# One matmul for the compressed-attention values, ScalarE writing the probabilities, heads of a sparse group spawned 8.5 apart

## The chip, the cores and the metric

The kernel runs on one core of one Trainium2 chip. TensorE (PE in the profile) multiplies, with a separate record for its weight loads (PEld); VectorE (DVE) and ScalarE (ACT) do the elementwise work, GpSimd (POOL) a little of it, and SyncE (SP) issues the loads. The metric is the device time of one execution in microseconds; lower is better.

## What is computed

A two-layer decoder on 256 tokens of width 2048. Layer 0 is a sparse attention (NSA) with 16 heads in 4 groups, layer 1 a differential attention; each is followed by a squared-ReLU MLP. The change touches only the sparse attention, whose head mixes three softmaxes. Cut to them:

```
kc, vc = compress(k_c, 0), compress(v_c, 1)        # 15 compressed keys and values per group
s_c = einsum(qr, kc) * scale                        # q without rope
p_c = masked_softmax(s_c, cmp_end <= t)
o_c = einsum(p_c, vc)
s_s = einsum(qo, k_g) * scale                       # q with rope, selected keys
p_s = masked_softmax(s_s, valid_s);  o_s = einsum(p_s, v_g)
p_w = masked_softmax(einsum(qo, kw) * scale, valid_w);  o_w = einsum(p_w, vw)
return g[..., 0:1] * o_c + g[..., 1:2] * o_s + g[..., 2:3] * o_w
```

With 256 tokens and 16 blocks to choose, all blocks are selected, so no gather is left in the kernel.

## The kernel before, in words

Every matrix product is made of three TensorE products of float32r parts: a value is split into a high part `h` (a rounded copy that ScalarE writes) and a low part `l` (VectorE: value minus `h`), and `mm3` computes hh + hl + lh. `split` is the helper (L150 to L156); weights go through it too (`raw` to `wh` and `wl`, L152 and L153, 128x1024 each).

The order of PE and SP is written by the program itself (`manual_schedule`, L158): the order in which the Python code emits matmuls is the order in which TensorE runs them. ACT, DVE and POOL get theirs from the framework's scheduler. The emission is driven by a small planner: `clock` is a number that each emitted matmul raises by its columns / 2400, tasks are generators in a heap, `yield d` puts a task back at clock + d, and `tick()`, which stands behind every few projection matmuls, runs a task that is due. So a head is a generator whose pieces are set between projection matmuls, and `WAIT_A` (L25) holds how far apart the planner puts them.

A sparse head (`nsa_head`, L597) has four pieces on PE:
- Q: four 128x128 transposes of its q without and with rope into one PSUM bank (tag `tp`); ACT writes `qth`, DVE `qtl`.
- S: the scores, 12 matmuls that read `qth` (the third reads `qtl`), into two `tp` banks. DVE adds the mask and takes the maxima (six operations, L632), ACT takes six exponentials with their sums (L635), DVE works out the gated reciprocals `den` and multiplies the six pieces by them (L641).
- P: eight transposes of the probabilities into two `tp` banks; ACT and DVE split them into `psh`, `psl` (first bank) and `pwh`, `pwl` (second).
- O: 15 matmuls into one `tp` bank; ACT and DVE split the result into `oth` and `otl` (tiles `big`).

Slots limit how many heads can be between two pieces: `s_q` 2 (Q to S), `s_s` 2 (S to P), `s_p` 1 (P to O). There are four `tp` banks, and all pieces use them. `heads` (L673) spawns the four heads of a group `WAIT_A[3]` apart; a group is spawned `WAIT_A[4]` after its q projection. The q projections of the four groups, and behind them the output projection (`out_proj`), supply the matmuls that stand between the pieces: 128x512, tiles `acc`, reading `wh` or `wl`.

The compressed values: `compress_tail` (L528) for `j == 1` makes each group's 15 (padded to 32) values four times over the 128 partitions, and splits them into `vch` and `vcl`. In O, three matmuls use partitions 96 to 127 of these (`cr`), against the same partitions of `psh`/`psl`, where the transposed compressed probabilities stand (the transposes of `sB[:, 160:288]` and `sB[:, 192:320]` end in those 32 columns).

Of the kernel before, what the change touches and what calls it, by code (L numbers as in the profile page):

```python
# [9 lines left out]
F32 = mybir.dt.float32  # L10
# [5 lines left out]
P = 128  # L16
# [5 lines left out]
NEG = -3.0e38  # L22
FLOOR = -1.0e38

WAIT_A = (2.0, 12.5, 4.0, 1.5, 7.0)  # L25

WAIT_B = (1.0, 8.5, 5.0, 5.5, 9.0, 7.0)
LAMBDA_INIT = 0.8 - 0.6 * math.exp(-0.3 * 1)
# [3 lines left out]
def kernel(  # L32
# [43 lines left out]
    def T(shape, tag, dt=F32):  # L76
        return (sm if tag in SMALL else sb).tile(shape, dt, tag=tag, name=name(tag), bufs=BUFS[tag])
# [23 lines left out]
    def spawn(gen, delay=0.0):  # L101
        task = Task(gen)
        put(task, delay)
        return task
# [32 lines left out]
    def mm(o, l, r, start, stop, shared=False):  # L137
        nc.tensor.matmul(o, lhsT=l, rhs=r, start=start, stop=stop, skip_group_check=shared)  # L138
        clock[0] += max(o.shape[-1], 256) / 2400.0
# [5 lines left out]
    def mm3(o, lh, ll, rh, rl, start, stop):  # L145
        mm(o, lh, rh, start, False)
        mm(o, lh, rl, False, False)
        mm(o, ll, rh, False, stop)

    def split(h, l, src, scale=None):  # L150
        if scale is None:
            nc.scalar.activation(h, src, AF.Copy)  # L152
            nc.vector.tensor_tensor(l, src, h.bitcast(F32), ALU.subtract)  # L153
        else:
            nc.scalar.activation(h, src, AF.Copy, scale=scale)
            nc.vector.scalar_tensor_tensor(l, src, scale, h.bitcast(F32), ALU.mult, ALU.subtract)  # L156
# [327 lines left out]
    def make_gates():  # L484
# [16 lines left out]
        nc.vector.tensor_scalar(gates, gates, 1.0, None, ALU.add)  # L501
        nc.vector.reciprocal(gates, gates)

    tG = spawn(make_gates())
    drain(tG)
    w2t = T([P, 2, 4, P], "q")
# [3 lines left out]

    kch = cp.tile([P, P], F32R, name="kch")
    kcl = cp.tile([P, P], F32R, name="kcl")
    vch = cp.tile([P, 4, P], F32R, name="vch")
    vcl = cp.tile([P, 4, P], F32R, name="vcl")

    def cmp_units(j, cps, first):
        def f(u):
# [10 lines left out]
    def compress_tail(cps, j):  # L528
        hs = T([120, 512], "sa")
        nc.scalar.activation(hs, cps[0:120, :], AF.Copy)  # L530
        yield 1.5
        tp = PT("tp")
        for k in range(4):
            transpose(tp[:, k * 120:(k + 1) * 120], hs[:, k * P:(k + 1) * P],
                                ident[0:120, 0:120])
        tv = tp[:, 0:480].rearrange("p (k c) -> p k c", k=4)
        u = T([P, 4, 60], "pwh")
        v = T([P, 4, 60], "pwl")
        nc.scalar.activation(v, tv[:, :, 60:120], AF.Copy)
        nc.vector.tensor_tensor(u, tv[:, :, 0:60], v, ALU.add)  # L540
        nc.gpsimd.tensor_tensor(v, u, u, ALU.mult)
        nc.vector.tensor_scalar(v, v, 0.044715, 1.0, ALU.mult, ALU.add)
        nc.gpsimd.tensor_tensor(v, v, u, ALU.mult)
        nc.scalar.activation(v, v, AF.Tanh, scale=math.sqrt(2.0 / math.pi))
        nc.vector.tensor_scalar(v, v, 1.0, None, ALU.add)
        gel = T([P, 4, 4, 32], "psh")
        nc.vector.memset(gel, 0.0)
        nc.gpsimd.tensor_tensor(gel.rearrange("p k h n -> p (k h) n")[:, :, 0:15],
                                u.rearrange("p k (h n) -> p (k h) n", n=15),
                                v.rearrange("p k (h n) -> p (k h) n", n=15), ALU.mult)  # L550
        gvs = []
        if j == 1:
            for h, tag in enumerate(("sa", "sa", "psl", "pwh")):
                gv = T([P, 4, 4, 32], tag)
                nc.gpsimd.tensor_copy(gv, gel[:, :, h, None, :].to_broadcast([P, 4, 4, 32]))
                gvs.append(gv)
        yield 10.0 if j == 0 else 16.0
        if j == 0:
            tp = PT("tp")
            for k in range(4):  # L560
                mm(tp[:, 0:128], w2[0][:, k, :], gel[:, k].rearrange("p h n -> p (h n)"), k == 0, k == 3)
            split(kch, kcl, tp[:, 0:128], half)
        else:
            tp = PT("tp")
            for h in range(4):
                gv = gvs[h]
                for k in range(4):
                    mm(tp[:, h * P:(h + 1) * P], gv[:, k].rearrange("p r n -> p (r n)"),
                       w2[1][:, k, :], k == 0, k == 3)
            split(vch.rearrange("p h d -> p (h d)"), vcl.rearrange("p h d -> p (h d)"), tp, half)  # L570

    half = cp.tile([P, 1], F32, name="half")
    nc.gpsimd.memset(half, 0.5)
# [23 lines left out]
    def nsa_head(hd, qr, qo):  # L597
        g, i = hd // 4, hd % 4
        yield from s_q.take()
        tp = PT("tp")  # L600
        for s_, src in ((0, qr), (2, qo)):
            for t in range(2):
                transpose(tp[:, (s_ + t) * P:(s_ + t + 1) * P], src[:, t, i * P:(i + 1) * P], ident)
        qh = T([P, 4, P], "qth", F32R)
        ql = T([P, 4, P], "qtl", F32R)
        split(qh.rearrange("p a q -> p (a q)"), ql.rearrange("p a q -> p (a q)"), tp)
        yield WAIT_A[0]
        yield from s_s.take()
        A = PT("tp")
        mm3(A, qh[:, 3, :], ql[:, 3, :], kkh[:, g], kkl[:, g], True, True)  # L610
        B = PT("tp")
        mm3(B[:, 0:256], qh[:, 2, :], ql[:, 2, :], kkh[:, g, 0:2], kkl[:, g, 0:2], True, True)
        n = slice(g * 32, (g + 1) * 32)
        mm3(B[:, 256:288], qh[:, 0, :], ql[:, 0, :], kch[:, n], kcl[:, n], True, True)
        mm3(B[:, 288:320], qh[:, 1, :], ql[:, 1, :], kch[:, n], kcl[:, n], True, True)
        s_q.give()
        sA = T([P, 512], "sa")
        sB = T([P, 320], "sbt")
        mx = T([P, 6], "mx")
        den = T([P, 6], "den")  # L620
        sv = sA.rearrange("p (a q) -> p a q", a=4)
        Av = A.rearrange("p (a q) -> p a q", a=4)
        spec = [
            (1, sB[:, 0:128], B[:, 0:128], cmask[:, 128:256], 1),
            (2, sB[:, 128:256], B[:, 128:256], cmask[:, 128:256], 2),
            (0, sB[:, 256:288], B[:, 256:288], vmask[:, 0:32], 0),
            (3, sB[:, 288:320], B[:, 288:320], vmask[:, 32:64], 0),
            (4, sv[:, 0::2, :], Av[:, 0::2, :], cm2, 1),
            (5, sv[:, 1::2, :], Av[:, 1::2, :], cm2, 2),
        ]  # L630
        for ix, so, si, mk, _ in spec:
            nc.vector.tensor_tensor_reduce(so, si, mk, 1.0, FLOOR, ALU.add, ALU.max, mx[:, ix:ix + 1])  # L632
        nc.vector.tensor_scalar(mx, mx, -scA, None, ALU.mult)
        for ix, so, si, mk, _ in spec:
            nc.scalar.activation(so, so, AF.Exp, bias=mx[:, ix:ix + 1], scale=scA, accum_out=den[:, ix:ix + 1])  # L635
        nc.vector.tensor_scalar(den, den, 1e-30, None, ALU.max)
        nc.vector.reciprocal(den, den)
        dv = den.rearrange("p (t b) -> p t b", t=2)
        nc.vector.tensor_tensor(dv, dv, gates[:, :, hd * 3:hd * 3 + 3], ALU.mult)
        for ix, so, si, mk, _ in spec:  # L640
            nc.vector.tensor_scalar(so, so, den[:, ix:ix + 1], None, ALU.mult)  # L641
        yield WAIT_A[1]
        yield from s_p.take()
        pts = []
        for br, srcs in enumerate((
            (sB[:, 0:128], sA[:, 0:128], sB[:, 160:288], sB[:, 192:320]),
            (sB[:, 128:256], sA[:, 128:256], sA[:, 384:512], sA[:, 256:384]),
        )):
            tp = PT("tp")
            for s_, src in enumerate(srcs):  # L650
                transpose(tp[:, s_ * P:(s_ + 1) * P], src, ident)
            ph = T([P, 512], ("psh", "pwh")[br], F32R)
            pl = T([P, 512], ("psl", "pwl")[br], F32R)
            split(ph, pl, tp)
            pts.append((ph, pl))
        s_s.give()
        yield WAIT_A[2]
        o = PT("tp")
        ds = slice(g * P, (g + 1) * P)
        cr = slice(96, 128)  # L660
        (ph, pl), (wph, wpl) = pts
        mm3(o[:, 0:256], vvh[:, 0, 0, ds], vvl[:, 0, 0, ds], ph[:, 0:256], pl[:, 0:256], True, False)
        mm3(o[:, 0:256], vch[cr, g, :], vcl[cr, g, :], ph[cr, 256:512], pl[cr, 256:512], False, False)
        mm3(o[:, 0:256], vvh[:, 1, 0, ds], vvl[:, 1, 0, ds], wph[:, 0:256], wpl[:, 0:256], False, False)
        mm3(o[:, 128:256], vvh[:, 1, 1, ds], vvl[:, 1, 1, ds], wph[:, 256:384], wpl[:, 256:384], False, False)
        mm3(o[:, 128:256], vvh[:, 0, 1, ds], vvl[:, 0, 1, ds], wph[:, 384:512], wpl[:, 384:512], False, True)
        s_p.give()
        split(oth[:, hd, :], otl[:, hd, :], o[:, 0:256])
# [364 lines left out]
```

## Time and profile before

| | |
|---|---|
| time, median of 3 runs (lowest to highest) | 2153.72 us (2153.3 to 2156.54) |
| the profiled execution: time, span | 2155.18 us, 2153.4 us |
| PE busy | 2127.6 us (99%), 10780 matmuls |
| DVE busy | 1334.7 us (62%) |
| ACT busy | 1082.9 us (50%) |
| chain that ended last | PE 93%, DVE 3%, DMA 1%, ACT 1% |
| mean DMA rate | 183 GB/s |

Busy is the share of the span in which an engine had an instruction running. Consecutive instructions of PE, ACT and DVE overlap in the records, so what one matmul costs the engine is read from the start of one to the start of the next, and not from its length. The sparse heads lie between about 222 and 402 us of the span, the heads of the differential attention between about 1237 and 1397 us.

### The profile page before, as it was taken

The numbers are of one execution on the slowest core, as the hardware profiler recorded it, in microseconds if no ns is written. First come the engines' busy times: TensorE is split into PE (matmuls) and PEld (weight loads), VectorE is DVE, ScalarE is ACT, GpSimd is POOL, SyncE is SP. The second block draws the span as 40 slices with busy tenths as digits, with TensorE's granted clock in tenths as the row PEclk, the third lists the DMA queues.
The fourth block names the chain that finished last, engine by engine and source line by source line (L and its number), as shares of the span: only waits on it lengthen the run. The fifth ranks groups of instructions, "written<-read, shape, count | busy, mean of one in ns | idle before, by whom it ended". The sixth has DMA issues, their size and how long they took to land.

```text
span 2153.4 us, 28803 instructions
## 1 busy us (share of the span) xinstructions
PE 2127.6 (99%) x10780; PEld 1796.6 (83%) x10780; DVE 1334.7 (62%) x2156; ACT 1082.9 (50%) x1737; POOL 81.3 (4%) x121
## 2 busy tenths in 40 slices
PE   8999999999999999999999999999999999999998
PEld 6878888888888888888888877888888888888886
DVE  5666777675556556655666578866546555655654
ACT  6665666464435434434555466654434434534443
POOL 0101100000000000000000111000000000000000
PEclk9999999999999999999999999999999999999999
DMA  7787433456666666666665543466566666666654
GB/s 241 238 271 242 128 98 95 149 172 191 191 190 190 196 195 185 196 191 191 188 190 187 188 138 126 128 191 190 190 193 185 195 195 189 187 200 187 194 192 142
DMA packets 204828, 394.45 MB, mean 183 GB/s; under 512 B 14176, under 2 KB 14368, under 8 KB 204560
## 3 DMA queue, kind: packets, MB, share of 16 engines
q1 hardware_dynamic: 203936, 390.51, 58.2%
q0 software_dynamic: 560, 2.02, 0.3%
q8 instruction: 84, 1.38, 0.3%
q14 instruction: 56, 0.46, 0.1%
q10 hardware_dynamic: 192, 0.08, 0.0%
HBM read 390.47 MB, written 2.10 MB: 182 GB/s over the span
## 4 chain that ended last, share of the span: by engine, by line
PE 93%; DVE 3%; DMA 1%; ACT 1%; issue 1%; POOL 0%; SPq 0%; POOLq 0%; DVEq 0%; ACTq 0%
PE acc L138 58%; PE tp L138 33%; PE tp L142 2%; DMA raw<-in_nsa_cmp_w_dram 1%; DVE wl L153 1%; ACT wh L152 1%; DMA raw<-in_nsa_w_in_dram 0%; ACT sbt L884 0%; ACT sa L884 0%; POOL sq L920 0%; DVE sbt L891 0%; DVE big L156 0%; DVE psl L153 0%; DVE sa L891 0%; DVE pwl L916 0%
## 5 line engine op out<-in xcount | busy, mean ns | idle before, releaser
L153 DVE TENSOR_TENSOR wl<-raw,wh 128x1024 fp32r<-128x1024 f32 x736 | 903.5, 1229 | 703.9 <-ACT wh L152 699.4
L152 ACT ACTIVATE wh<-raw 128x1024 fp32r<-128x1024 f32 x736 | 778.5, 1059 | 819.3 <-PE acc L138 478.8
L138 PE MATMUL acc<-wh,big 128*128 128x512 f32 (+1 forms) x1600 | 543.2, 400 | 1.5 <-ACT wh L152 1.5
L138 PE MATMUL acc<-wh,kv 128*128 128x512 f32 x1280 | 397.2, 390 | 0.0
L138 PE MATMUL tp<-big,wh 128*128 128x512 f32 (+1 forms) x1040 | 359.5, 392 | 0.0
L138 PE MATMUL acc<-big,wh 128*128 128x512 f32 x1024 | 358.1, 394 | 0.0
L138 PEld LDWEIGHTS acc<-wh,big 128*128 128x128 f32 (+1 forms) x1600 | 301.6, 189 | 60.9 <-ACT wh L152 1.9
L138 PE MATMUL acc<-wl,big 128*128 128x512 f32 (+1 forms) x832 | 326.3, 392 | 0.5 <-DVE wl L153 0.5
L138 PE MATMUL tp<-big,wl 128*128 128x256 f32 (+1 forms) x1040 | 288.9, 280 | 0.0
L138 PE MATMUL acc<-big,wl 128*128 128x256 f32 x1024 | 286.9, 280 | 0.0
L138 PEld LDWEIGHTS acc<-wh,kv 128*128 128x128 f32 x1280 | 240.3, 188 | 50.0
L138 PE MATMUL acc<-wl,kv 128*128 128x512 f32 x640 | 249.0, 389 | 0.0
L138 PE MATMUL tp<-wh,kv 128*128 128x512 f32 x768 | 237.4, 389 | 0.0
L138 PEld LDWEIGHTS tp<-big,wh 128*128 128x128 f32 (+1 forms) x1040 | 194.2, 187 | 44.0
L138 PEld LDWEIGHTS acc<-big,wh 128*128 128x128 f32 x1024 | 192.3, 188 | 43.7
L138 PEld LDWEIGHTS tp<-big,wl 128*128 128x128 f32 (+1 forms) x1040 | 194.9, 188 | 0.0
L138 PEld LDWEIGHTS acc<-big,wl 128*128 128x128 f32 x1024 | 193.0, 188 | 0.2
L138 PEld LDWEIGHTS acc<-wl,big 128*128 128x128 f32 (+1 forms) x832 | 157.1, 189 | 28.6 <-DVE wl L153 1.0
L138 PEld LDWEIGHTS tp<-wh,kv 128*128 128x128 f32 x768 | 144.1, 188 | 29.9
L138 PE MATMUL tp<-wl,kv 128*128 128x512 f32 x384 | 149.4, 389 | 0.0
L138 PEld LDWEIGHTS acc<-wl,kv 128*128 128x128 f32 x640 | 120.2, 188 | 24.5
L152 ACT ACTIVATE kv<-q 128x256 fp32r<-128x256 f32 x128 | 50.0, 412 | 73.5 <-DVE q L745 73.5
(183 smaller groups left out, 1418.5 us busy)
## 6 DMA issues: line engine op xcount, KB each, us to landing
raw<-in_mlp_w_up_dram SPq DMA_DIRECT2D x256, 512.0 KB, 3.9
raw<-in_mlp_w_down_dram SPq DMA_DIRECT2D x256, 512.0 KB, 4.0
raw<-in_nsa_w_in_dram SPq DMA_DIRECT2D x80, 512.0 KB, 4.5
raw<-in_nsa_cmp_w_dram SPq DMA_DIRECT2D x32, 512.0 KB, 5.0
raw<-in_nsa_w_out_dram SPq DMA_DIRECT2D x32, 512.0 KB, 3.7
raw<-in_diff_w_q_dram SPq DMA_DIRECT2D x32, 512.0 KB, 3.7
raw<-in_diff_w_out_dram SPq DMA_DIRECT2D x32, 512.0 KB, 3.7
raw<-in_kv_w_shared_dram SPq DMA_DIRECT2D x16, 512.0 KB, 3.6
```

What stands on the lines that cost most here:

```text
L138: nc.tensor.matmul(o, lhsT=l, rhs=r, start=start, stop=stop, skip_group_check=shared)
L142: nc.tensor.transpose(o, i, idn)
L152: nc.scalar.activation(h, src, AF.Copy)
L153: nc.vector.tensor_tensor(l, src, h.bitcast(F32), ALU.subtract)
```

## The change

It has four parts. The spacing of a group's heads in the planner, `WAIT_A[3]`, becomes 8.5 in place of 1.5. ACT's exponential of the compressed scores reads each score four times over and writes 4 x 32 columns (`sc`), its sum is four times as large, and the gate of that branch is multiplied by 4 once. The compressed values are kept in one tile `vcs` whose partitions hold h, l, h, l in blocks of 32, and the transposed probabilities hold their high part in partitions 0 to 63 and their low part in 64 to 127: one matmul over 128 partitions takes the place of three over 32. The split of that bank is written out: one copy by ACT, two subtractions by DVE (128x256, and 64x256 in place).

```
-WAIT_A = (2.0, 12.5, 4.0, 1.5, 7.0)
+WAIT_A = (2.0, 12.5, 4.0, 8.5, 7.0)
...
+        gc = gates.rearrange("p t (h b) -> p t h b", b=3)[:, :, :, 0]
+        nc.vector.tensor_scalar(gc, gc, 4.0, None, ALU.mult)
...
-    vch = cp.tile([P, 4, P], F32R, name="vch")
-    vcl = cp.tile([P, 4, P], F32R, name="vcl")
+    vcs = cp.tile([P, 4, P], F32R, name="vcs")
...
-            split(vch.rearrange("p h d -> p (h d)"), vcl.rearrange("p h d -> p (h d)"), tp, half)
+            vf = vcs.rearrange("p h d -> p (h d)")
+            nc.scalar.activation(vf, tp, AF.Copy, scale=half)
+            for r in (slice(32, 64), slice(96, 128)):
+                nc.vector.scalar_tensor_tensor(vf[r], tp[r], half[r], vf[r].bitcast(F32), ALU.mult, ALU.subtract)
...
-        sB = T([P, 320], "sbt")
+        sB = T([P, 576], "sbt")
+        sc = sB[:, 256:512].rearrange("p (t r n) -> p t r n", t=2, r=4)
...
-        for ix, so, si, mk, _ in spec:
-            nc.scalar.activation(so, so, AF.Exp, bias=mx[:, ix:ix + 1], scale=scA, accum_out=den[:, ix:ix + 1])
+        es = []
+        for ix, so, si, mk, br in spec:
+            if br == 0:
+                so, eo = so[:, None, :].to_broadcast([P, 4, 32]), sc[:, ix // 3]
+            else:
+                eo = so
+            es.append((ix, eo))
+            nc.scalar.activation(eo, so, AF.Exp, bias=mx[:, ix:ix + 1], scale=scA, accum_out=den[:, ix:ix + 1])
...
-        for ix, so, si, mk, _ in spec:
-            nc.vector.tensor_scalar(so, so, den[:, ix:ix + 1], None, ALU.mult)
+        for ix, eo in es:
+            nc.vector.tensor_scalar(eo, eo, den[:, ix:ix + 1], None, ALU.mult)
...
-            (sB[:, 0:128], sA[:, 0:128], sB[:, 160:288], sB[:, 192:320]),
+            (sB[:, 0:128], sA[:, 0:128], sB[:, 256:384], sB[:, 384:512]),
...
-            split(ph, pl, tp)
+            if br == 0:
+                nc.scalar.activation(ph, tp, AF.Copy)
+                nc.vector.tensor_tensor(pl[:, 0:256], tp[:, 0:256], ph[:, 0:256].bitcast(F32), ALU.subtract)
+                lo = ph[64:128, 256:512]
+                nc.vector.tensor_tensor(lo, tp[64:128, 256:512], lo.bitcast(F32), ALU.subtract)
+            else:
+                split(ph, pl, tp)
...
-        mm3(o[:, 0:256], vch[cr, g, :], vcl[cr, g, :], ph[cr, 256:512], pl[cr, 256:512], False, False)
+        mm(o[:, 0:256], vcs[:, g, :], ph[:, 256:512], False, False)
```

The first place is PE in the last sparse head: in the order before, its Q is `tp_3538` and its S begins with `tp_3711`; `acc` rows are projection matmuls.

```order
L142 MATMUL tp_3538<-cst,q_3139 128x128 x2
L142 MATMUL tp_3538<-cst,q_3142 128x128 x2
L138 MATMUL acc_3269<-wh_3404,big_1616 128x512
...
L142 MATMUL tp_3690<-cst,sbt_3493 128x128
...
L138 MATMUL acc_3646<-wh_3531,big_1617 128x512
L138 MATMUL tp_3711<-kv_611,qth_3543 128x512
L138 MATMUL tp_3711<-kv_612,qth_3543 128x512
```

The same head in the order now: Q is `tp_3629`, S begins with `tp_3663`, and P of the head before it (`tp_3641`, `tp_3651`) stands between them.

```order
L142 MATMUL tp_3629<-cst,q_3124 128x128 x2
L142 MATMUL tp_3629<-cst,q_3127 128x128 x2
L138 MATMUL acc_3286<-wh_3475,big_1616 128x512
L138 MATMUL acc_3286<-wl_3476,big_1616 128x512
L138 MATMUL acc_3286<-wh_3475,big_1617 128x512
L142 MATMUL tp_3641<-cst,sbt_3442 128x128
...
L142 MATMUL tp_3651<-cst,sa_3441 128x128 x3
L138 MATMUL acc_3287<-wh_3475,big_1616 128x512
L138 MATMUL acc_3287<-wl_3476,big_1616 128x512
L138 MATMUL acc_3287<-wh_3475,big_1617 128x512
L138 MATMUL tp_3663<-kv_611,qth_3634 128x512
```

In the order before, 88 rows lie between this head's Q and its S, now 11. S of the last head was at row 1705 and is now at row 1658; S of the first was at 878 and is now at 879.

The second place is ACT around the same head's `qth`, first before:

```order
L635 ACTIVATE sbt_3493,den_3495<-sbt_3493,mx_3494 128x128 x2
L635 ACTIVATE sbt_3493,den_3495<-sbt_3493,mx_3494 128x32 x2
L635 ACTIVATE sa_3492,den_3495<-sa_3492,mx_3494 128x2x128 x2
L152 ACTIVATE wh_3652<-raw_3400 128x1024
L152 ACTIVATE qth_3543<-tp_3538 128x512
L152 ACTIVATE big_1616<-tp_3556 128x256
```

and now:

```order
L649 ACTIVATE sbt_3559,den_3561<-sbt_3559,mx_3560 128x128
L152 ACTIVATE wh_3717<-raw_3467 128x1024
L649 ACTIVATE sbt_3559,den_3561<-sbt_3559,mx_3560 128x128 x3
L649 ACTIVATE sa_3558,den_3561<-sa_3558,mx_3560 128x2x128 x2
L152 ACTIVATE qth_3634<-tp_3629 128x512
L670 ACTIVATE psh_3646<-tp_3641 128x512
```

In both, `qth` stands behind the six exponentials of the head before it.

The third place is DVE around `qtl` of the third head (hd 2), first before:

```order
L632 ISA sa_1982,mx_1984<-tp_1968,cst 128x2x128
L632 ISA mx_1984 128x1
L636 TENSOR_SCALAR den_1927<-den_1927 128x6
L633 TENSOR_SCALAR mx_1984<-mx_1984 128x6
L153 TENSOR_TENSOR qtl_2017<-tp_2011,qth_2016 128x512
L637 RECIPROCAL den_1927<-den_1927 128x6
```

and now:

```order
L653 TENSOR_TENSOR den_2028<-den_2028,gates 128x6
L655 TENSOR_SCALAR sbt_2026<-sbt_2026,den_2028 128x128 x4
L655 TENSOR_SCALAR sa_2025<-sa_2025,den_2028 128x2x128 x2
L671 TENSOR_TENSOR psl_2105<-tp_2099,psh_2104 128x256
L153 TENSOR_TENSOR wl_2206<-raw_1990,wh_2205 128x1024
L673 TENSOR_TENSOR psh_2104<-tp_2099,psh_2104 64x256
L153 TENSOR_TENSOR pwl_2115<-tp_2109,pwh_2114 128x512
L153 TENSOR_TENSOR qtl_2127<-tp_2121,qth_2126 128x512
```

`qtl` of this head stood ahead of the multiplications of its neighbour, and now stands behind them and behind the splits of another head's probabilities. The orders of SP and POOL are the same in both kernels.

## Rows read from the trace of the kernel before

**Rows 1.** The page's busy table: engine, busy us (share of the span), instructions.

```profile
PE 2127.6 (99%) x10780; PEld 1796.6 (83%) x10780; DVE 1334.7 (62%) x2156; ACT 1082.9 (50%) x1737; POOL 81.3 (4%) x121
```

**Rows 2.** Windows: us, busy of PE, PEld, DVE, ACT, POOL, clock, DMA share, GB/s.

```profile
240.00:400.00 160.00, 160.00 (x939) 137.02 (x939) 119.22 (x404) 99.57 (x270) 9.75 (x19) 1.00 0.34 103
1237.00:1397.00 160.00, 153.74 (x765) 123.95 (x764) 130.65 (x405) 103.00 (x289) 21.31 (x32) 0.99 0.42 131
```

**Rows 3.** Timeline of PE in one O: start, us, engine, line, operation, tiles.

```profile
300.18 0.28 PE L138 MATMUL tp<-psh,kv 128*128 128x256 f32 x1
300.38 0.38 PE L138 MATMUL tp<-psh,vch 32*128 32x256 f32 x1
300.61 0.28 PE L138 MATMUL tp<-psl,vch 32*128 32x256 f32 x1
300.73 0.28 PE L138 MATMUL tp<-psh,vcl 32*128 32x256 f32 x1
300.94 0.38 PE L138 MATMUL tp<-pwh,kv 128*128 128x256 f32 x1
301.16 0.28 PE L138 MATMUL tp<-pwl,kv 128*128 128x256 f32 x1
```

**Rows 4.** Timeline of all engines, 267.7 to 276 us: one head's Q to S.

```profile
267.87 0.60 PE L142 MATMUL tp<-cst,q 128*128 128x128 f32 x4
268.22 0.48 PE L138 MATMUL acc<-wh,big 128*128 128x512 f32 x1
268.54 0.39 PE L138 MATMUL acc<-wl,big 128*128 128x512 f32 x1
...
271.40 0.57 ACT L152 ACTIVATE qth<-tp 128x512 fp32r<-128x512 f32 x1
...
272.04 0.68 DVE L153 TENSOR_TENSOR qtl<-tp,qth 128x512 fp32r<-128x512 f32 x1
...
275.47 0.62 PE L138 MATMUL tp<-kv,qth 128*128 128x512 f32 x2
...
275.93 0.40 PE L138 MATMUL tp<-kv,qtl 128*128 128x512 f32 x1
```

**Rows 5.** The same for another head, 361.8 to 369 us.

```profile
361.99 0.60 PE L142 MATMUL tp<-cst,q 128*128 128x128 f32 x4
...
367.42 0.61 DVE L641 TENSOR_SCALAR sa<-sa,den 128x256 f32<-128x256 f32 x2
367.95 0.68 DVE L153 TENSOR_TENSOR qtl<-tp,qth 128x512 fp32r<-128x512 f32 x1
```

**Rows 6.** The instructions on `qth`: duration ns min/median/max, first and last start.

```profile
L138 PE MATMUL tp<-kcl,qth x32: 262/263/263, 226.3 to 379.8; 128*128 128x32 f32 x32
```

**Rows 7.** Waits of DVE, 240 to 400 us: total us, times, longest.

```profile
DVE wl L153 <- ACT wh L152: 18.7, 25, 1.9
DVE den L636 <- ACT sa L635: 15.1, 14, 1.1
```

**Rows 8.** Groups by form, 240 to 400 us: busy us, mean ns, idle before.

```profile
L635 ACT ACTIVATE sbt<-sbt,mx 128x128 f32<-128x128 f32 x28 | 10.8, 387 | 1.6 <-DVE mx L633 1.6
...
L635 ACT ACTIVATE sbt<-sbt,mx 128x32 f32<-128x32 f32 x28 | 8.6, 306 | 0.0
...
L153 DVE TENSOR_TENSOR psl<-tp,psh 128x512 fp32r<-128x512 f32 x16 | 11.0, 685 | 2.9 <-ACT psh L152 2.9
...
L641 DVE TENSOR_SCALAR sbt<-sbt,den 128x128 f32<-128x128 f32 x28 | 6.7, 281 | 0.2
L153 DVE TENSOR_TENSOR big<-tp,big 128x256 fp32r<-128x256 f32 x15 | 6.1, 405 | 0.2 <-ACT big L152 0.2
L641 DVE TENSOR_SCALAR sbt<-sbt,den 128x32 f32<-128x32 f32 x28 | 5.4, 234 | 0.0
```

**Rows 9.** Windows around one idle stretch of PE in the differential heads.

```profile
1337.00:1339.70 2.70, 1.37 (x8) 0.91 (x9) 2.22 (x13) 1.44 (x7) 0.69 (x1) 1.00 0.64 204
1339.70:1343.10 3.40, 3.40 (x14) 2.86 (x13) 1.80 (x8) 2.46 (x10) 0.00 (x0) 0.53 0.03 7
```

More of the change, by code (lines that the diff above doesn't have):

```diff
@@ L625, in nsa_head @@
             (2, sB[:, 128:256], B[:, 128:256], cmask[:, 128:256], 2),
-            (0, sB[:, 256:288], B[:, 256:288], vmask[:, 0:32], 0),
-            (3, sB[:, 288:320], B[:, 288:320], vmask[:, 32:64], 0),
+            (0, sB[:, 512:544], B[:, 256:288], vmask[:, 0:32], 0),
+            (3, sB[:, 544:576], B[:, 288:320], vmask[:, 32:64], 0),
             (4, sv[:, 0::2, :], Av[:, 0::2, :], cm2, 1),
@@ L659, in nsa_head @@
         ds = slice(g * P, (g + 1) * P)
-        cr = slice(96, 128)
         (ph, pl), (wph, wpl) = pts
         mm3(o[:, 0:256], vvh[:, 0, 0, ds], vvl[:, 0, 0, ds], ph[:, 0:256], pl[:, 0:256], True, False)
-        mm3(o[:, 0:256], vch[cr, g, :], vcl[cr, g, :], ph[cr, 256:512], pl[cr, 256:512], False, False)
+        mm(o[:, 0:256], vcs[:, g, :], ph[:, 256:512], False, False)
         mm3(o[:, 0:256], vvh[:, 1, 0, ds], vvl[:, 1, 0, ds], wph[:, 0:256], wpl[:, 0:256], False, False)
```

## The prediction, before the changed kernel ran

> **What bounds the kernel now.** I read the busy table first: PE is busy for 2127.6 of 2153.4 us [rows 1], so only what changes PE's own work, or makes it wait, can move the time. Then the windows, to see whether that also holds where the change is [rows 2]: in the stretch of the sparse heads, 240 to 400 us, PE is busy for all 160 us, while DVE has work for 119.2 us and ACT for 99.6. No piece of a sparse head is late for PE. The stretch of the differential heads is the contrast to keep in mind: the same way of interleaving, DVE at 130.65 of 160 us, and there PE is idle for 160 - 153.7 = 6.3 us.
>
> **The matmuls that go.** In the timeline of one O the reader is to look at starts, not lengths [rows 3]. An ordinary step of 256 columns is 0.12 us (300.61 to 300.73). Around the three 32-row matmuls the steps are 0.20, 0.23, 0.12, 0.21 and 0.22: the last full-height matmul before them, the three, and the first full-height one behind them, 0.98 us in all. With one matmul over 128 partitions in their place there are three ordinary steps, 0.36 us. That is 0.62 us a head and 16 x 0.62 = 9.9 us for the kernel, all of it on PE, which sets the end there. The Trainium skill has the reason: TensorEngine Tiling, Key Properties, says that a change of the tiling mode drains the engine. The trace agrees, with 0.20 and 0.22 us where 0.12 is ordinary; without that rule the two matmuls saved would be 16 x 2 x 0.12 = 3.8 us.
>
> **The small edits.** Per head, two exponentials grow from 32 to 128 columns, 2 x (387 - 306) = 162 ns on ACT, and two multiplications likewise, 2 x (281 - 234) = 94 ns on DVE [rows 8]. The subtraction `psl` of 685 ns becomes one of 128x256 (the nearest row is `big`, also from PSUM, 405 ns) and one of 64x256, not shown in this trace, which I take at the same 405: +125 ns; at its least, if half the partitions took no time at all, it is 280 ns less. ACT gets 0.16 us and DVE 0.2 us more a head. With DVE at 75% and ACT at 62% of the stretch that alone would be hidden; if the cover goes it counts in full, 16 x 0.2 = 3.2 us. The gates' factor and the two subtractions for `vcs` are three instructions, once, before the heads: below 1 us even if all of it showed.
>
> **The spacing.** This is the part that can cost. PE has no time of its own in it, but it decides how long the pieces' ACT and DVE work may take before PE stands at the next piece.
>
> From Q to S. Before, Q ran early: in the order the last head has 88 rows between its Q and its S; now it has 11. What must fit between is `qth` on ACT and `qtl` on DVE. When they stand behind the neighbour's six exponentials, this takes 4.85 us from the start of Q (267.87) to the end of `qtl` (272.04 + 0.68); S came at 275.47 and its third matmul, the first that reads `qtl`, at 275.93, so nobody noticed [rows 4]. When `qtl` also stands behind the neighbour's multiplications it takes 361.99 to 368.63, 6.64 us [rows 5]. The cover now, by steps from the same rows: four transposes 0.35, the projection matmul behind them 0.32, each further one 0.23, and 0.46 more to the third matmul of S [rows 4].
> - Second head: twelve projection matmuls, so 0.35 + 0.32 + 11 x 0.23 + 0.46 = 3.66 us, behind exponentials: 4.85 - 3.66 = 1.2 us of waiting.
> - Third head: the same 3.66, but `qtl` behind multiplications and the splits of P (the order of DVE shows it): 6.64 - 3.66 = 3.0.
> - Fourth head: Q, three matmuls, another Q, six matmuls, 3.41 us, the same queue: 3.2.
> - The last two: Q, three matmuls, the eight transposes of P (2 x 0.35), three matmuls, 0.35 + 0.78 + 0.70 + 0.78 + 0.46, about 3.1 us, behind exponentials (the order of ACT): 1.7 each.
>
> Together 10.8 us. Queued behind a late `qtl` on DVE are the next head's maxima, and behind a late S everything on PE.
>
> The other ten periods. From the first to the last head's scores are (379.8 - 226.3) / 15 = 10.2 us a head [rows 6]. Now PE's queue holds less between two heads: S of the last head stood 827 rows behind that of the first, and stands 779 behind it. Of these 48 rows 30 are the 32-row matmuls, the other 18 are projection matmuls now run after the heads, so a period of PE is 10.2 - 0.62 - 18 x 0.23 / 15 = 9.3 us. DVE still has 119.2 / 15.7 = 7.6 us of work in each, plus 0.2, and that is 84% of 9.3, above the 82% at which the differential heads already make PE wait [rows 2]. What decides is DVE's idle time: 15.1 us in 14 waits of `den` for the last exponential, 1.1 a head, belong to the chain and cannot be squeezed; 18.7 us, 1.2 a head, are waits for `wh`, which can [rows 7]. If all idle time stays, a period needs 10.2 us and PE waits 0.9; if the waits for `wh` vanish, 9.0 or 9.1 us are needed and PE waits for nothing. I take the upper end, since the stretch with the nearest share of DVE does wait: 10 x 0.9 = 9 us.
>
> The clock. In the differential heads PE was busy for only 1.37 of the 2.70 us before 1339.7, and the granted clock fell to the 1.2 GHz level for the next 3.4 us (0.53 on the mean), which loses 3.4 x 0.47 = 1.6 us [rows 9]. I count that once.
>
> **Sum.** -9.9 + 10.8 + 9 + 1.6 = +11.5 us. The profiled execution took 2155.18 us (span 2153.4 and 1.8 around it), so 2166.7; the median of the runs is 1.46 us below that execution, hence 2165.
>
> **Rivals.**
> 1. The queues keep up, and the 9.9 us stay: 2143.8 us. For it: PE waits nowhere in the stretch now, and ACT and DVE have idle time in sum. Against it: the waits are a matter of order, not of sums, and rows 4 shows `qth` starting 3.2 us after its transposes. The Trainium skill sharpens that in a sentence of its own: TensorE: Matmul & The Clock Gate, Part 1, calls ACT's and DVE's queues strictly first in, first out, so a split that PE wants cannot pass a neighbour's softmax; were it able to, this rival would be the forecast.
> 2. PE waits, but no more than in the differential heads, 6.3 us [rows 2], up to as much as is gained: 2153.7 - 9.9 + 6.3 = 2150.1 to 2153.7 us. For it: these heads stand 9.0 apart in their own table of waits, close to 8.5, with Q just ahead of S. Against it: a sparse head has six maxima, exponentials and multiplications where they have four.
> 3. The clock: each of the five waits of 1.2 to 3.2 us takes it down, not one of them: 4 x 1.6 = 6.4 us more, about 2172 us. For it: rows 9. Against it: in the differential heads only one stretch of 160 us shows the lower clock.
> That the change doesn't do what it says is ruled out by the order: the 32-row matmuls are gone and Q has moved.
>
> **Chances.** Forecast 0.58, with its own range 2158 to 2172, slower throughout (the low end leaves out most of the ten periods' 9 us). Rival 1: 0.09, faster. Rival 2: 0.20, of which 0.03 is faster and 0.17 within 0.2%, 4.3 us, which is about what a measurement of this kernel tells from no change. Rival 3: 0.13, slower. So faster 0.12, same 0.17, slower 0.71. The range is 2152 to 2174: it leaves out the first rival, the lower part of the second and the top of the third, 0.19.
>
> **What the profile will show.** Right: steps of 0.12 us through all of O; a window over the sparse heads with PE idle for some 20 us, in front of matmuls that read `qth` and `qtl` above all in the second to fourth and in the last two heads, and the rest at O or at a `tp` bank; DVE above 80% there; the stretches up to 200 us and behind 450 us unchanged. The gain is wrong if the matmul on `vcs` or the one behind it still takes 0.2 us. The loss is wrong if PE's busy time fills the window as before: then the time is near 2144. If PE waits at other pieces than S, the price was right for another reason.

## The result, and the profile after

| | before | after |
|---|---|---|
| time, median of 5 runs on the same chip (lowest to highest) | 2154.57 us (2153.3 to 2156.54) | 2171.21 us (2170.06 to 2174.43) |
| ratio, 95% interval | | 1.0078 [1.0067, 1.0089] |
| profiled span | 2153.4 us | 2169.9 us |

The change makes the kernel 0.8% slower. The prediction said 2165 us, slower, with a range of 2152 to 2174.

The busy table of after, to be read against [rows 1]: PE has the same busy time although 32 matmuls are gone, and its share of the span falls from 99 to 98%. A part of this busy time is matmuls that run at the lower clock (shown further down).

```profile
PE 2128.7 (98%) x10748; PEld 1796.6 (83%) x10748; DVE 1339.4 (62%) x2174; ACT 1084.9 (50%) x1737; POOL 81.7 (4%) x121
```

The windows of after (us, then busy time of PE, PEld, DVE, ACT and POOL, the granted clock, DMA share, GB/s): the sparse heads, and the differential heads, which now lie 16.5 us later. They answer to [rows 2]. PE stood idle for nothing in the first window before, and for 160 - 145.9 = 14.1 us now, at a mean clock of 0.97; the differential heads are as before (153.71 for 153.74 us).

```profile
240.00:400.00 160.00, 145.90 (x843) 123.44 (x842) 114.81 (x416) 99.10 (x276) 10.37 (x19) 0.97 0.28 87
1253.50:1413.50 160.00, 153.71 (x766) 123.97 (x765) 130.80 (x406) 103.10 (x289) 21.29 (x32) 0.99 0.41 131
```

DVE's busy time in the window went down, not up. The engine that PE waits for is busy for 72% of the stretch. What it does with the rest is in the view of waits of after, 240 to 400 us (engine, line waited for: total us, times, longest), first PE, then DVE:

```profile
PE tp L138 <- ACT qth L152: 3.4, 3, 1.6
PE tp L138 <- DVE qtl L153: 3.3, 2, 1.8
PE tp L138 <- DVE psh L673: 2.2, 2, 1.1
PE tp L138 <- DVE pwl L153: 1.6, 1, 1.6
PE tp L142 <- POOL q L361: 1.4, 1, 1.4
PE tp L138 <- DVE den L651: 1.0, 1, 1.0
```

```profile
DVE den L650 <- ACT sa L649: 22.7, 14, 2.7
DVE wl L153 <- ACT wh L152: 13.7, 11, 3.2
```

The largest entry is DVE's own: at `den` it stands for the last exponential of its head, 22.7 us in 14 waits where it was 15.1 in 14 [rows 7]. Everything that PE wants from DVE stands behind it meanwhile. ACT's own waits in the same window show the other half of this, first before, then after:

```profile
ACT sbt L635 <- DVE mx L633: 1.6, 1, 1.6
```

```profile
ACT sbt L649 <- DVE mx L641: 13.5, 12, 3.2
```

The two engines stand waiting for each other: ACT's first exponential of a head waits for DVE's maxima, and DVE at `den` for ACT's last exponential.

One of the waits in detail: the timeline of after, DVE and PE, at the third head's S (start, us, engine, line, operation, tiles, idle before and its releaser).

```profile
244.08 1.06 DVE L655 TENSOR_SCALAR sbt<-sbt,den 128x128 f32<-128x128 f32 x4
...
245.06 0.60 DVE L655 TENSOR_SCALAR sa<-sa,den 128x256 f32<-128x256 f32 x2
...
245.59 0.41 DVE L671 TENSOR_TENSOR psl<-tp,psh 128x256 fp32r<-128x256 f32 x1
...
245.92 1.21 DVE L153 TENSOR_TENSOR wl<-raw,wh 128x1024 fp32r<-128x1024 f32 x1
...
246.42 0.73 PE L138 MATMUL tp<-kv,qth 128*128 128x512 f32 x2 [0.40 <-ACT qth L152]
...
247.16 0.43 DVE L673 TENSOR_TENSOR psh<-tp,psh 64x256 fp32r<-64x256 f32 x1
247.62 0.69 DVE L153 TENSOR_TENSOR pwl<-tp,pwh 128x512 fp32r<-128x512 f32 x1
248.23 0.68 DVE L153 TENSOR_TENSOR qtl<-tp,qth 128x512 fp32r<-128x512 f32 x1
...
248.96 0.50 PE L138 MATMUL tp<-kv,qtl 128*128 128x512 f32 x1 [1.81 <-DVE qtl L153]
```

The reader is to follow DVE downward: the neighbour's multiplications, `psl`, a weight split that PE does not wait for here, the new second subtraction, `pwl`, and only then `qtl`. S began as soon as `qth` was ready. By starts, the third matmul of S comes 248.96 - 246.42 = 2.54 us behind the first, where 0.46 is ordinary [rows 4]: the wait costs 2.1 us, somewhat more than the 1.81 that the idle column shows. Taken so over all of PE's steps from 200 to 450 us (each step less the usual one of its shape), the waits are 20.5 us at full clock, and the steps at the lower clock are together 6.1 us too long. With the 9.9 us that O saves: -9.9 + 20.5 + 6.1 = +16.7 us; the span grew by 16.5.

The saving itself is there. The timeline of one O in after: all steps are 0.11 to 0.13 us, where [rows 3] have 0.20, 0.23, 0.12, 0.21 and 0.22.

```profile
320.42 0.28 PE L138 MATMUL tp<-psl,kv 128*128 128x256 f32 x1
320.54 0.28 PE L138 MATMUL tp<-psh,kv 128*128 128x256 f32 x1
320.66 0.28 PE L138 MATMUL tp<-psh,vcs 128*128 128x256 f32 x1
320.77 0.28 PE L138 MATMUL tp<-pwh,kv 128*128 128x256 f32 x1
320.90 0.28 PE L138 MATMUL tp<-pwl,kv 128*128 128x256 f32 x1
```

The instructions on `qth` show what became of it, against [rows 6]: the last head's scores come at 389.3 us, 9.5 us later than before.

```profile
L138 PE MATMUL tp<-kcl,qth x32: 262/263/376, 225.9 to 389.3; 128*128 128x32 f32 x32
```

The clock. Windows of after ahead of and in the three places where the granted clock is at its 1.2 GHz level; the columns are as above.

```profile
237.00:250.20 13.20, 11.00 (x58) 8.72 (x56) 9.35 (x29) 8.18 (x20) 1.21 (x4) 1.00 0.50 152
250.20:253.60 3.40, 3.40 (x15) 3.11 (x15) 1.52 (x12) 1.63 (x4) 0.00 (x0) 0.50 0.02 7
300.00:304.80 4.80, 2.21 (x12) 1.30 (x10) 4.15 (x14) 2.92 (x9) 0.00 (x0) 1.00 0.33 109
304.80:311.60 6.80, 6.80 (x26) 5.93 (x25) 3.56 (x16) 2.51 (x8) 0.00 (x0) 0.50 0.03 9
399.00:403.80 4.80, 3.20 (x18) 2.28 (x16) 4.03 (x8) 1.16 (x2) 0.00 (x0) 1.00 0.49 136
403.80:407.20 3.40, 3.40 (x12) 2.72 (x11) 0.42 (x1) 0.38 (x1) 0.00 (x0) 0.50 0.32 116
```

Each time PE had waits in the stretch ahead (in 300 to 304.8 us it was busy for 2.21 of 4.80), and then runs at half speed for 3.4, 6.8 and 3.4 us: 13.6 us together. The sparse heads of before have none.

### The profile page after: what moved, and what is told of

It reads as the page before. It is cut to its first block, busy times and chain, and to the rows that moved or that the text cites. A ratio compares the mean times of both kernels' runs of the same rounds, so it can differ in the third digit from the quotient of the medians.

```text
span 2169.9 us, 28769 instructions
## 1 busy us (share of the span) xinstructions
PE 2128.7 (98%) x10748; PEld 1796.6 (83%) x10748; DVE 1339.4 (62%) x2174; ACT 1084.9 (50%) x1737; POOL 81.7 (4%) x121
## 4 chain that ended last, share of the span: by engine, by line
PE 87%; DVE 6%; ACT 3%; DMA 2%; issue 1%; POOL 0%; SPq 0%; DVEq 0%; POOLq 0%; ACTq 0%
PE acc L138 55%; PE tp L138 31%; DVE wl L153 2%; PE tp L142 1%; ACT wh L152 1%; DMA raw<-in_nsa_cmp_w_dram 1%; ACT sbt L649 1%; ACT sa L649 1%; DMA raw<-in_nsa_w_in_dram 1%; DVE sbt L655 0%; ACT sbt L904 0%; ACT sa L904 0%; DVE qtl L153 0%; DVE pwl L153 0%; DVE sa L655 0%
```

## The experiments

The theory: PE waits for splits that stand in DVE's queue behind softmax work of other heads, and the price is set by what stands in that queue, so the parts of the change act on each other. The rivals: the spacing alone is to blame, or the shorter O on PE, or pieces that the planner put in worse places, or ACT and the banks.

Each was run several times in turn with the kernel before, which took 2154.2 to 2155.0 us (medians) beside them. "Waits" are PE's steps as above, 200 to 450 us.

**The two halves of the change, each alone.** Stack without spacing:

```
-WAIT_A = (2.0, 12.5, 4.0, 8.5, 7.0)
+WAIT_A = (2.0, 12.5, 4.0, 1.5, 7.0)
```

> The changed kernel with the spacing back at 1.5 (everything else as changed). Theory: the stacked matmul gives PE 9.9 us, and the loss came in with the spacing; without it PE waits in the sparse heads for 5 us at most (a period of PE is 10.2 - 0.62 = 9.6 us against 7.8 us of DVE work), so 2144.7 to 2150 us, faster than before, O in steps of 0.12 us throughout, no stretch at the 1.2 GHz level among the sparse heads. Rival: the copies that ScalarE writes and the split in two pieces make the heads late by themselves; then PE waits for 10 us or more here too, and the time is 2154 us or above.

Measured: 2148.58 us, ratio 0.9969 [0.9958, 0.9981]. And the spacing without the stack (the kernel before with 8.5):

> The kernel before with the spacing 8.5 and nothing else. If the waits hang on the spacing alone (Q just ahead of S, as the prediction priced five heads), they come here too: 10.8 to 20 us, 2165 to 2175 us. If they come from the spacing together with the shorter period of PE (0.62 us less work of its own per head), most of them are hidden here by the 32-row matmuls: 2 to 7 us of waiting, 2157 to 2162 us.

Measured: 2159.07 us, ratio 1.002 [1.0011, 1.0029]. The window of the stack alone, and its waits (PE's longest, and DVE's longest, from two answers), 240 to 400 us:

```profile
240.00:400.00 160.00, 157.54 (x937) 135.90 (x936) 124.71 (x428) 102.98 (x274) 10.01 (x19) 1.00 0.35 108
```

```profile
PE tp L138 <- DVE pwl L153: 1.4, 2, 1.2
...
DVE den L650 <- ACT sa L649: 13.9, 11, 2.4
```

The same of the spacing alone:

```profile
240.00:400.00 160.00, 155.98 (x915) 132.02 (x914) 119.12 (x411) 98.70 (x278) 9.68 (x19) 1.00 0.31 97
```

```profile
PE tp L138 <- DVE qtl L153: 2.5, 4, 1.0
...
DVE den L636 <- ACT sa L635: 22.0, 12, 2.5
```

Waits are 4.5 us with the stack alone and 5.5 with the spacing alone, and neither has a stretch at 1.2 GHz there. Against the runs of before the halves give -5.8 and +4.7, together -1.1; the whole change gives +16.6. So some 17.7 us arise only where both meet. The spacing alone already holds DVE at `den` for 22.0 us, as in the whole change; PE then waits little as long as nothing else is added.

**Is it the spacing as such?** The changed kernel with O set later behind P, at 8.5:

```
-WAIT_A = (2.0, 12.5, 4.0, 8.5, 7.0)
+WAIT_A = (2.0, 12.5, 5.5, 8.5, 7.0)
```

> The changed kernel, spacing 8.5, with the wait between P and O raised from 4.0 to 5.5 in the planner's table: every O, and with it the next head's P, moves later by some six projection matmuls. Theory (pieces too close together for ACT and DVE): waits of PE fall from 20.5 us to 5 to 10, and the stretches at the lower clock from three to none or one: 2150 to 2160 us. Rival (the spacing as such, Q just ahead of S, is all of it): the waits in front of S stay, 2165 us or more.

Measured: 2155.61 us, ratio 1.0 [0.9991, 1.0009]. Waits fall to 8.2 us, with one stretch of 6.8 us at 1.2 GHz. At the same spacing 15.6 us are gone, so the spacing as such is not the price. Two things can have taken the waits away, and the run does not separate them. The pieces stand at other places in the queues, and a later O also puts more projection matmuls between the heads. Between the scores of the first and the last head the traces have 354 of them (`acc`) before, 330 in the change and 417 here: (417 - 330) x 0.23 / 15 = 1.3 us more of PE's own work a head, as cover.

**Idle time and the clock.** In the changed kernel, matmuls that do nothing were put where two of the longer waits were:

```
+        def fill(o, n):
+            for _ in range(n):
+                nc.tensor.matmul(o, lhsT=kkh[:, g, 0, :], rhs=kkh[:, g], start=True, stop=True)
+        if hd == 7:
+            fill(A, 7)
...
+        if hd == 2:
+            fill(B, 8)
```

> The changed kernel with 15 matmuls of 128x512 that compute nothing (on loaded keys, into a bank that is started afresh behind them), 8 in the third head's S and 7 ahead of the eighth head's, where PE waited 2.0 and 1.6 us: work in the place of idle time. If idle time of PE is what takes the clock down, the stretches at the lower level behind 250 and 305 us go (10.2 us of them, half of which is lost): 2166 to 2168 us, 3 to 5 us faster than the changed kernel. If the clock falls for another reason, they stay, and the time is 2171 us or up to 3 us more.

Measured: 2170.53 us, ratio 1.0071 [1.0058, 1.0083], between the two expectations. In the profiled execution the lower clock at 250 and 305 us is gone, as it should be if the idle time there had brought it on. The stretch at 405 us, which answers to the change's third, is still there, and one came at 388 us, of 3.4 us each. One execution doesn't show the cause (see the last section: the same waits can come with and without such a stretch), and in time the run decides nothing.

**DVE's queue.** The changed kernel without the six multiplications of each head (the branches are summed unnormalised):

```
-        for ix, eo in es:
-            nc.vector.tensor_scalar(eo, eo, den[:, ix:ix + 1], None, ALU.mult)
```

> The changed kernel, spacing 8.5, without the six multiplications of a head's probabilities by the gated reciprocals (the branches are summed unnormalised). That takes 1.6 us of DVE's work from each of the 16 heads and shortens DVE's queue behind the softmax; PE's order stays. Theory (PE waits since splits stand in DVE's queue behind a neighbour's softmax): the 20.5 us of waits fall to 7 or less, and with them the stretches at 1.2 GHz: 2145 to 2155 us. Rival (the waits come from ACT's queue, or from too few banks and slots, and DVE is only busy beside it): no more than 5 us of them go, 2165 to 2171 us.

Measured: 2147.54 us, ratio 0.9966 [0.9954, 0.9978]. The window and what is left of PE's waits:

```profile
240.00:400.00 160.00, 157.80 (x949) 137.11 (x948) 109.58 (x348) 106.38 (x288) 9.41 (x19) 1.00 0.34 105
```

```profile
PE tp L142 <- POOL q L361: 1.4, 1, 1.4
PE tp L138 <- DVE qtl L153: 0.8, 1, 0.8
```

The waits for `qth`, `psh`, `pwl` and `den` are gone, and with them the lower clock. In the timeline above, the six multiplications take 245.59 - 244.08 = 1.5 us by starts, 16 x 1.5 = 24 us in all, and the time falls by 23.7. PE's order is that of the change, so PE has no more cover than there. So work on an engine that is busy for 72% of the stretch can count. That the two numbers nearly agree is no price for a microsecond of it: waits and lower clock cost the change 20.5 + 6.1 = 26.6 us, and no run can give back more. Nothing was taken from ACT's own work or added to the `tp` banks, which were the rival.

**Q earlier.** The changed kernel with 4.0 instead of 2.0 from Q to S (`WAIT_A[0]`):

> The changed kernel, spacing 8.5, with 4.0 instead of 2.0 from Q to S. Theory of the prediction (a fair part of the loss is S standing too close behind Q): the waits on qth and qtl, 5.8 us in the trace, go, with some of the lower clock: 2160 to 2166 us. Rival (what is late is DVE's and ACT's queue as a whole, and PE waits at the next piece instead): 2168 to 2175 us.

Measured: 2163.78 us, ratio 1.0042 [1.0029, 1.0054]. PE's waits, 240 to 400 us, the first two:

```profile
PE tp L138 <- DVE den L651: 5.4, 4, 1.6
PE tp L138 <- DVE den L653: 1.8, 1, 1.8
```

`qth` and `qtl` have left the list, and 7.4 us of time with them: the theory's size. A part of it may be cover again, since 375 projection matmuls now stand between the first and the last scores, for 330. The rest has not gone; S now waits for DVE to get past `den`, and the waits sum to 15 us.

**The second subtraction, taken away and added.** First, the changed kernel without the 64x256 subtraction (the low half of the stacked part stays a copy of the high one):

```
-                lo = ph[64:128, 256:512]
-                nc.vector.tensor_tensor(lo, tp[64:128, 256:512], lo.bitcast(F32), ALU.subtract)
```

> The changed kernel, spacing 8.5, without the second subtraction of a head's first probability bank (64x256, in place; the low half of the stacked compressed part stays a copy of the high one). It takes only some 0.4 us of DVE's work from a head, 4 per cent of its period. Theory A (the second subtraction matters by its place: O needs it, and a 128x1024 weight split can stand between the two subtractions in DVE's queue): waits fall by a third or more, 2152 to 2163 us. Theory B (only the amount of DVE's work counts): 16 x 0.4 = 6.4 us of work at most, and by the share of it that shows as waits 1 to 4 us: 2167 to 2171 us.

Measured: 2163.35 us, ratio 1.0035 [1.0023, 1.0048], a third of a microsecond beyond theory A and far from B; waits 10.8 us in the profiled execution, which was a short one of its runs (span 2156.7). These runs lie far apart, 2158.44 to 2165.53 us, the two short ones at a mean granted clock of 0.996 and the others at 0.993 or 0.994, so the distance to the change is known to a few microseconds only. Then the reverse: the kernel before, spacing 8.5, with a second subtraction. It writes values that are there already, but O reads a part of them and so has to wait for it.

```
             split(ph, pl, tp)
+            if br == 0:
+                lo = slice(64, 128), slice(256, 512)
+                nc.vector.tensor_tensor(pl[lo], tp[lo], ph[lo].bitcast(F32), ALU.subtract)
```

> The kernel before with the spacing 8.5 alone (2159.1 us in an earlier run), and a second subtraction of 64x256 behind each head's psl, which writes the same low parts again. PE's work is unchanged. Theory (in the changed kernel the second DVE instruction of the split is what turned a harmless spacing into a costly one: it sits in DVE's queue and other work gets between the two): waits rise by 6 us or more, 2165 to 2175 us. Rival (what made the spacing costly is that PE's own O became shorter, so less time passes on PE): 0 to 3 us for 16 x 0.4 us of work on an engine with room, 2159 to 2162 us.

Measured: 2180.87 us, ratio 1.0122 [1.0108, 1.0136], 21.8 us above the spacing alone, and more than the theory's upper end. The window, PE's longest waits, and the end of one of them (DVE and PE):

```profile
240.00:400.00 160.00, 146.63 (x809) 123.54 (x809) 111.12 (x392) 90.07 (x257) 9.06 (x18) 0.94 0.28 86
```

```profile
PE tp L138 <- DVE qtl L153: 6.3, 3, 2.8
PE tp L142 <- DVE big L153: 2.6, 1, 2.6
```

```profile
360.13 0.68 DVE L153 TENSOR_TENSOR pwl<-tp,pwh 128x512 fp32r<-128x512 f32 x1
360.84 0.43 DVE L657 TENSOR_TENSOR psl<-tp,psh 64x256 fp32r<-64x256 f32 x1
361.30 1.23 DVE L153 TENSOR_TENSOR wl<-raw,wh 128x1024 fp32r<-128x1024 f32 x1
362.56 0.69 DVE L153 TENSOR_TENSOR qtl<-tp,qth 128x512 fp32r<-128x512 f32 x1
363.31 0.50 PE L138 MATMUL tp<-kv,qtl 128*128 128x512 f32 x1 [2.84 <-DVE qtl L153]
```

0.43 us of DVE's work a head, 6.9 us in all, cost 21.8: the waits went from 5.5 to 17.5 us, and stretches at 1.2 GHz, 20.5 us long together, cost 9.2 more.

**Amount, or the second instruction as such?** The run without the second subtraction again, with the first one over all 512 columns:

```
-                nc.vector.tensor_tensor(pl[:, 0:256], tp[:, 0:256], ph[:, 0:256].bitcast(F32), ALU.subtract)
+                nc.vector.tensor_tensor(pl, tp, ph.bitcast(F32), ALU.subtract)
```

> The run without the second subtraction again (spacing 8.5, the low half of the stacked part stays a copy of the high one), but with psl written over all 512 columns, so that the split of that bank takes one DVE instruction of about 0.68 us, as in the kernel before; the columns beyond 256 are read by nothing. In the other runs it takes 0.42 us (one instruction), 0.84 us (two, the changed kernel) and 1.11 us (two, the kernel before with a second subtraction). Theory 1 (that there is a second instruction is what costs, by what stands between the two): as without it, 2158 to 2165 us. Theory 2 (what counts is how much DVE work stands in a head's period, and steeply so): between that run and the changed kernel, 2166 to 2171 us.

Measured: 2168.3 us, ratio 1.0058 [1.0044, 1.0071]: theory 2, the amount, among the runs with one matmul. The expectation behind the run without the second subtraction, that its place is what matters, is not borne out there. Five runs at 8.5, by DVE's work on that bank:

| O's compressed part | DVE on the first bank, us a head | time, us |
|---|---|---|
| three matmuls of 32 rows | 0.68 (spacing alone) | 2159.07 |
| three matmuls of 32 rows | 0.68 + 0.43 | 2180.87 |
| one matmul | 0.42 | 2163.35 |
| one matmul | 0.68 | 2168.3 |
| one matmul | 0.41 + 0.43 (the change) | 2171.21 |

The three runs with one matmul lie nearly on a line: 7.9 us of time for 0.42 us a head, 6.7 us of work in all, or 1.2 us for each. The other two don't lie on it: there 6.9 us of work cost 21.8, or 3.2 for each. So the amount alone does not explain that pair, and the place in the queue is not ruled out for it.

**Two rivals on the interaction.** O with as many matmuls as before (the compressed branch counts three times), and the planner's number raised as if it had them:

```
         mm(o[:, 0:256], vcs[:, g, :], ph[:, 256:512], False, False)
+        mm(o[:, 0:256], vcs[:, g, :], ph[:, 256:512], False, False)
+        mm(o[:, 0:256], vcs[:, g, :], ph[:, 256:512], False, False)
```

> The changed kernel, spacing 8.5, with the matmul on the stacked values done three times over, so that PE has as many matmuls in O as before (the compressed branch counts three times). That is 16 x 2 x 0.12 = 3.8 us more on PE, and as much more cover for ACT and DVE. Theory (DVE's queue is what is late): at most the 3.8 us of waits are filled, 2169 to 2176 us. Rival (the shorter O took PE's cover away, and that made the 17.7 us by which the two parts together cost more than each alone): waits and lower clock fall by 12 us or more, 2160 to 2164 us.

Measured: 2176.1 us, ratio 1.0102 [1.0086, 1.0117]. That is 4.9 us above the change, where the two matmuls themselves take 3.8, and a tenth above the theory's upper end. Two ordinary matmuls more in O don't bring the cover back.

```
         mm(o[:, 0:256], vcs[:, g, :], ph[:, 256:512], False, False)
+        clock[0] += 2 * 256 / 2400.0
```

> The changed kernel, spacing 8.5, with the planner's number raised in O by two further matmuls of 256 columns that aren't issued, so that the planner sets the pieces of the heads as if O still had three matmuls there. Theory (queues): the waits stay, 2166 to 2174 us. Rival (the pieces fell into worse places since O counts for less in the planner's number): back to the waits of the spacing alone, 5 to 6 us, so 2145 to 2155 us.

Measured: 2169.16 us, ratio 1.0071 [1.0058, 1.0084]. That the pieces fell into worse places because O counts for less is ruled out as the main cause. The run also has 351 projection matmuls between the first and the last scores, as many as the spacing alone, so the change's smaller number is not the main cause either.

**A version that beats both.** The stack with the old spacing, P and O set later:

```
-WAIT_A = (2.0, 12.5, 4.0, 8.5, 7.0)
+WAIT_A = (2.0, 13.0, 5.0, 1.5, 7.0)
```

> The changed kernel with the heads back at 1.5, and P and O each set later behind the piece before them (13.0 instead of 12.5, 5.0 instead of 4.0). Theory (the stack is worth its 9.9 us, and what was left in the stack-only run, 2148.6 us, are 4.5 us of waits of PE in front of O for splits that DVE has not reached): later P and O leave at most 1.5 us of them, so 2144 to 2147 us, faster than both kernels. Rival (those 4.5 us belong to the shorter period of a head, wherever its pieces stand): 2148 to 2151 us.

Measured: 2145.5 us (2143.81 to 2146.02), ratio 0.9954 [0.9942, 0.9967]. Busy table, the window, and DVE at `den`:

```profile
PE 2116.5 (99%) x10748; PEld 1789.5 (83%) x10748; DVE 1339.8 (62%) x2174; ACT 1083.8 (51%) x1737; POOL 81.4 (4%) x121
```

```profile
240.00:400.00 160.00, 159.90 (x934) 138.60 (x933) 126.90 (x414) 102.13 (x263) 8.92 (x18) 1.00 0.39 119
```

```profile
DVE den L650 <- ACT sa L649: 8.5, 7, 1.3
```

DVE has the same work a head, it is busy for 79% of the window, and PE waits for next to nothing. DVE stands at `den` for 8.5 us and not 22.7, and ACT no longer waits for the maxima at all. A part of this can be cover: 447 projection matmuls stand between the first and the last scores, (447 - 330) x 0.23 / 15 = 1.8 us more a head than in the change. The heads' scores come (394.7 - 227.6) / 15 = 11.1 us apart, although the planner's number is 1.5. So the run kept neither the period of a head nor the places of its pieces, and does not decide between its theory and its rival.

## Why the prediction was right, and where it wasn't

**The matmuls that go: right.** 9.9 us were counted. The version without waits is 2155.03 - 2145.5 = 9.5 us faster than before. Its span is 9.7 us shorter; 1.6 us of that are the stretch at the lower clock in the differential heads [rows 9], which is missing in this execution, and its sparse heads begin 1.3 us later, so the stretch from 222 to 450 us by itself gives 9.4. Single steps are as foretold, the first full-height matmul behind the compressed one included. The Trainium skill's rule (TensorEngine Tiling, Key Properties) that a change of tiling mode drains the engine agrees with the gain too: by the count of matmuls alone it would have been 3.8 us.

**What the loss is: right in kind.** PE waits for splits that are late in DVE's and ACT's queues, though neither engine is busy all the time; taking work out of DVE's queue brings the time back (2147.54 us without multiplications).

**"The small edits": wrong.** They were costed at nothing, hidden by DVE's idle time, with 3.2 us at most if the cover goes. This step failed: the cover went. What the change itself adds to the split, from 0.68 to 0.84 us a head, is worth 2171.21 - 2168.3 = 2.9 us, nearly the whole 3.2, and the larger exponentials and multiplications, which no run took away by themselves, come on top. The queue as a whole is dearer still: 0.42 us a head taken from the split is worth 7.9 us, and 0.43 added to the spacing alone costs 21.8. How much of the 26.6 us of waits and lower clock the small edits make is not shown (see Open). The cover that the prediction named, a quarter of DVE's time, was time in which DVE stood at `den` or at `wl` with the splits queued behind. The new `psl` and the 64x256 subtraction were sized right (408 and 428 ns for the estimated 405 each).

**"The other ten periods": right in sign, 9 us for some 14.6, by a wrong constant.** The 14.6 are what is left of the 20.5 us when the five heads' 5.9 are taken away. By PE's starts the larger ones stand at O (5.1 us in all), at the second bank of S (3.7), at Q (2.0) and at the eighth head's S (1.6). The 1.1 us a head at `den` "belong to the chain and cannot be squeezed", but they could grow: 22.7 / 14 = 1.6 in after, and 22.0 / 12 = 1.8 with the spacing alone. And most of DVE's waits for `wh` stayed, 13.7 us of 18.7. The projection matmuls that left the heads were 24 by the traces (354 to 330) and not 18, which makes PE's period 0.1 us shorter still.

**"From Q to S": the sum too high, 10.8 for 5.9.** The third head waited 2.5 us (3.0 predicted), the last two 1.8 and 1.5 (1.7 each). The second waited for nothing. The fourth neither: the next group's first Q, which stands between its Q and S, itself waited 1.6 us for POOL's rope (`q`, L361), and that was time enough for `qtl`. Run with an earlier Q, these waits go.

**"The clock": mis-sized, 1.6 for 6.1 us.** One stretch was counted; there were 13.6 us of them. The prediction's third rival had that mechanism, but not every wait brought a stretch: one came behind the longest, of 2.1 us, and none behind two of 1.8.

So -9.9 + 20.5 + 6.1 stands where -9.9 + 19.8 + 1.6 was written. The waits agree in total because the terms that were too high and too low met. The prediction also never priced the spacing alone. Two of its terms, 10.8 us from Q to S and 1.6 for the clock, don't rest on the shorter O, so they should have shown there; that run lost 4.7 us in all, and had no stretch at the lower clock. The size was right in the sum only, which is luck. Of the signs that the prediction named, DVE above 80% did not come (72%), and its last one, PE waiting at other pieces than S, holds for some 7 us at O and Q: to that extent the price was right for another reason.

**Open.** From the spacing alone to the run with one matmul and one wide subtraction the time rises by 9.2 us although DVE's split is equal: PE's O is 9.9 us shorter, and the larger exponentials and multiplications add 0.16 us on ACT and 0.1 on DVE a head. Ordinary matmuls added to O did not undo it. That 6.9 us of work cost 21.8 on one side of this step and 6.7 us only 7.9 on the other is open too. With each edit ACT's and DVE's order also changes somewhat, and its part was not separated from that of the amount.

## What to carry to other kernels

An engine with idle time can still have no room: look at what it stands waiting for and at what is queued behind that wait, and don't cost work that is added to such a queue at nothing: here a microsecond of it cost 1.2 or 3.2. Price the halves of a change apart and then together, since here -5.8 and +4.7 us made +16.6. When pieces are interleaved, leave slack between a piece's split and its use, and put independent matmuls there: the version with P and O later, with 447 projection matmuls among the heads and not 330, gained 9.5 us. Which of the two did it was not separated.

## What the runs showed of the hardware

- In the changed kernel the granted clock fell to 1.2 GHz although PE was never idle for more than about 2 us at once: after 11.00 busy of 13.20 us, 2.21 of 4.80, and 3.20 of 4.80. It came back after 3.4 or 6.8 us (10.2 in the run with the subtraction added).
- The same waits can come with a stretch at 1.2 GHz and without. Ahead of the stretch in the differential heads [rows 9], PE's two long steps are 0.8 and 1.5 us in all 14 profiled executions of this case; the stretch follows in six of them (before and after among these) and not in eight. It costs 1.6 us, so this much of a difference between two profiled spans can be chance.
- A subtraction from PSUM over 64 partitions takes as long as over 128, by the groups by form of after, 240 to 400 us (busy us, mean ns):

```profile
L673 DVE TENSOR_TENSOR psh<-tp,psh 64x256 fp32r<-64x256 f32 x14 | 6.0, 428 | 0.3
...
L671 DVE TENSOR_TENSOR psl<-tp,psh 128x256 fp32r<-128x256 f32 x14 | 5.7, 408 | 0.0
```

  For 512 columns it is 685 [rows 8], so the two cost 0.15 us more than one whole.
- A wait costs PE more than its idle time in the trace: 2.1 us by starts where the idle column shows 1.81.
